# A kernel planner that may place GpSimd's sums and scalings on VectorE, and makes GpSimd wait for a VectorE operation that it held up

## The chip, the cores and the metric

The kernel runs on one core of a Trainium2 chip. The metric is the device time of one execution in microseconds, the median of several. The core's engines, by their names in the profile, are PE (TensorE, matrix products; PEld is its weight load), DVE (VectorE), ACT (ScalarE), POOL (GpSimd) and SP (SyncE, which issues the transfers). Each runs its own list of instructions in order, and they wait for each other by semaphores.

## What is computed

One layer of a bidirectional encoder over 2048 tokens of width 1024: windowed attention with 16 query heads and 4 key heads of width 64 (each query block of 128 tokens sees 384 keys), then a gated feed-forward part of width 2816. Around each part stand RMS norms and a shift, scale and gate from a conditioning vector. The reference, cut:

```python
mod = (silu(c) @ ada_w + ada_b);  sh1, sc1, g1, sh2, sc2, g2 = split(mod, 6)
h = rmsnorm(x, mix_norm_pre) * (1 + sc1) + sh1
q, k, v = split(h @ w_qkv)
logits = where(window, q @ k.T * dh**-0.5 + rel_bias, -1e30)
p = softmax(concat([logits, sink]))[..., :-1]
x = x + g1 * rmsnorm((p @ v) @ w_o, mix_norm_post)
h = rmsnorm(x, ffn_norm_pre) * (1 + sc2) + sh2
a, b = split(h @ ffn_w_in)
x = x + g2 * rmsnorm((silu(a) * b) @ ffn_w_out, ffn_norm_post)
```

All is float32. A product is made of three matmuls on rounded parts: each operand is split into `hi`, its rounded copy (made on ACT), and `lo`, the rest (a subtraction on DVE or POOL), and hi x hi, hi x lo and lo x hi are summed in a PSUM bank (`three`, line 782, and `split`, line 788).

## The kernel before

The kernel has two layers of code. `encoder_layer` (line 708) writes down the whole computation as a list of operations, each with a fixed engine. A recorder takes the list, a planner orders it, and the result is emitted; for this reason nearly every instruction carries the same line, 693, in the profile, and one goes by the names of the tiles.

*The work, in order of time.* (1) Norm, query, key and value products of the first chunk of 512 tokens, with the weights split as they come (`w_piece`, line 898, on POOL) and the modulation reduced on DVE (`ada`). (2) Attention in 64 units (`Unit`): four score products, a sum with the bias on DVE (`pr<-bank`), the exponential on ACT, a scaling of each of the four heads' rows by the reciprocal sum on POOL (`pr<-pr,rs`, line 1076), transposes on PE, ACT and DVE copies (`phi`, `plo`), the value product, and its reading from the bank (`low` on ACT, `of` on DVE). Between the units PE gets other work as filler: the remaining query, key and value products, then, from the middle on, the output projection (`ol`, `wo`) with its norms and residuals, whose sums (`y`, `yacc`, `xacc`, lines 1131 to 1146 and 1206) are POOL's. (3) The feed-forward's first product, in two halves of the tokens and 22 column tiles each. It is done with seven products instead of eight (a 2x2 block scheme): DVE makes sums and differences of weights (`s_i`, `wiri`), ACT and DVE split them (`ws_i`, `wa_i`), and DVE combines the seven results from the banks (`u_i`, `p_i`, `b_i`). POOL multiplies the two gates (`p_i<-p_i,u_i`, line 1443) and makes half of the differences for the next product (`differences`, line 1148). (4) The second product, in the same scheme and several parts (`ws_o`, `wa_o`, `z`); four of the final combinations of each block are POOL's (line 1572), the others DVE's. (5) Squares, norms, and the output (`zsq`, `nrz`, `zx`).

The PSUM banks are few: in attention two for the scores, three for the transposes, one for the value product and two for filler; in the feed-forward six.

*What sets the order.* `record` (line 176) gives each operation its costs (`cost`, line 233): the time for which it occupies its engine, its latency, and whether it uses the SBUF access that DVE and POOL share (`port`: every POOL operation except custom ones; on DVE, operations of over 128 columns with two SBUF inputs, and copies and scalings within SBUF). `forward` (line 330) plays the engines forward: each has a heap of operations that are ready (`now`) and of those that become ready (`soon`); the engine that can begin earliest takes its most urgent operation. An operation with `port` begins at the earliest 60 ns before the other engine's operation with `port` ends. `backward` (line 569) computes urgencies from the result, `replay` (line 509) plays an order again under random delays of the transfers, and `schedule` (line 632) repeats this 18 times and keeps the order with the shortest replay. `HOP` (line 75) is the planner's delay from one engine to another, 105 ns to POOL. `emit` (line 656) writes the instructions in that order, each on its engine; where the planner made one operation wait for another on purpose (`extra`), it adds a dependence.

So the planner knows that the two engines exclude each other, but in the program nothing says which goes first.

Of the kernel before, what the change touches and what calls it, by code (L numbers as in the profile page):

```python
# [76 lines left out]
class Op:  # L77
    __slots__ = ("i", "eng", "fn", "args", "kw", "reads", "writes", "occ", "lat", "port", "table", "tiles", "pred", "succ",
                 "start", "end", "put", "prio", "npred", "ready", "ins", "bytes",
                 "wire", "out", "wait", "extra")  # L80

# [52 lines left out]
class Recorder:  # L134
# [41 lines left out]
    def record(self, eng, fn, args, kw):  # L176
        op = Op()
# [14 lines left out]
        elif fn == "matmul":  # L192
            op.writes = [(op.writes[0][0], (3, (1 << P) - 1))]
        self.cost(op, [x for j, x in aps if j in out], [x for j, x in aps if j not in out])
        op.pred = {}
# [18 lines left out]
        self.ops.append(op)  # L214
        return op

    def gap(self, q, op):
# [112 lines left out]
    def forward(self, ahead, spare):  # L330
# [8 lines left out]
        for o in ops:  # L339
            o.npred, o.ready, o.put, o.wait, o.extra = len(o.pred), 0.0, 0, None, []  # L340
# [3 lines left out]
        port, moved = {"dve": 0.0, "pool": 0.0}, 0  # L344
        lanes, dma, table = [0.0] * 8, 0.0, None
# [20 lines left out]
        def offer(o):  # L366
            ready = o.ready
            for b in o.tiles:
# [8 lines left out]
        def drop(heap, o):  # L377
            if o in heap[0]:
                heapq.heappop(heap)
            else:  # L380
                heap.pop(next(k for k, x in enumerate(heap) if o in x))
                heapq.heapify(heap)

        def wake(t):
            for u in (t, *t.later):
                if u.parked:
                    again, u.parked = u.parked, []
                    for o in again:
                        offer(o)

        for o in ops:
            if not o.npred:
                offer(o)
        while n < len(ops):
            best = None
            for e in ENGINES:
                t, nw, sn = clock[e], now[e], soon[e]
                if e == "sp":
                    t = max(t, lanes[0])
                while sn and sn[0][0] <= t:  # L400
                    r, p, i, o = heapq.heappop(sn)
                    heapq.heappush(nw, (p, i, o, r))
                if nw:
                    item, begin, src = nw[0], t, nw
                elif sn:
                    item, begin, src = sn[0], sn[0][0], sn
                    item = (item[1], item[2], item[3], item[0])
                else:
                    continue
                o = item[2]  # L410
                ask = begin
                if o.port:
# [4 lines left out]
            if e == "dve" and o.port and src is now[e] and begin > clock[e] + 150:  # L417
                other = [x for x in now[e] if not x[2].port]
                if other:
                    item = min(other)  # L420
                    o, begin = item[2], clock[e]
                    ask = begin
            if ahead and e in ("act", "dve", "pool") and o.put < 4:
                wait, by = 0.0, None
                for g in (e, *({"dve": ("pool",), "pool": ("dve",)}.get(e, ()) if o.port else ())):
                    for r, p, i, y in soon[g]:
                        if g != e and not y.port:
                            continue
                        if r < begin + o.occ and max(begin - o.prio, begin + o.occ - p) > max(r - p, r + y.occ - o.prio) + 50:
                            w = r + (y.lat + HOP[e] if g != e else 1.0)  # L430
                            if w > wait:
                                wait, by = w, y if g != e else None
                if wait:
                    drop(src, o)
                    o.put += 1
                    if by is not None:
                        o.wait = by
                    heapq.heappush(soon[e], (wait, o.prio, o.i, o))
                    continue
            if e == "act" and o.table and o.table != table:  # L440
                stay = [x for x in now[e] if x[2].table in (None, table)]
                near = [x for x in soon[e] if x[3].table == table and x[0] < begin + 900]
                if stay and near:
                    item = min(stay)
                    o, src = item[2], now[e]
                elif near:
                    x = min(near)
                    item, src, o, begin = (x[1], x[2], x[3], x[0]), soon[e], x[3], max(begin, x[0])
            drop(src, o)
            again = False  # L450
# [10 lines left out]
            y = o.wait  # L461
            if y is not None and y.npred < 0 and max(clock[e], o.ready) <= y.start + 20:
                o.extra = [y]
                begin = max(begin, y.end + HOP[e])
            if e == "act" and o.table and o.table != table:
                table = o.table
                begin += 1283
# [10 lines left out]
            else:  # L478
                end = begin + o.lat
                if o.port:  # L480
                    port[e] = begin + o.occ
            o.npred = -1
            clock[e] = begin + o.occ + (late if e == "sp" else 0)
            o.start, o.end = begin, end
# [17 lines left out]
            for q in o.succ:  # L502
                q.npred -= 1
                q.ready = max(q.ready, begin if o.eng == q.eng == "pe" else end + (HOP[q.eng] if o.eng != q.eng else 30))
                if not q.npred:
                    offer(q)
# [125 lines left out]
    def schedule(self, rounds):  # L632
# [8 lines left out]
        for i in range(rounds):  # L641
# [4 lines left out]
            if best is None or real < best[1]:  # L646
                best = order, real, {b: b.slot for b in self.bufs.values()}, {o: o.extra for o in order if o.extra}
            if prio:
                for o in order:
                    o.prio = prio[o]  # L650
        self.slots, self.extra = best[2:]
        return best[0]
# [3 lines left out]
    def emit(self, nc, tc, order, outside):  # L656
# [1106 lines left out]
```

## Time and profile before

| | |
|---|---|
| median of 3 runs | 2058.2 us (2055.8 to 3376.76) |
| profiled execution, own time | 2063.44 us |
| its span, first to last instruction | 2061.7 us |
| granted TensorE clock, mean | 0.991 |
| instructions on DVE, ACT, POOL | 2933, 2122, 687 |
| DMA | 396.33 MB, mean 192 GB/s |

How to read it: the page gives busy times for the whole span; the windows view gives them by stretch, with the granted clock, and is what shows where PE is not busy; the view of waits and the timelines say what ended a gap. An arrow `<-` within brackets names what the engine waited for, with the time.

The chain of work that ended last goes through PE's matmuls for 54% of the span (936.73 us in one piece, from 870.39 us). POOL's instructions and their time by kind:

| POOL instruction | count | mean, ns |
|---|---|---|
| scaling `pr<-pr,rs`, 128x384 | 256 | 603 |
| small copy `pr<-nsink`, 128x4 | 64 | 237 |
| gate product `p_i<-p_i,u_i`, 128x512 | 44 | 1613 |
| gate product `u_i<-u_i,b_i`, 128x512 | 44 | 1483 |
| sums `z<-z,z`, 128x512 | 32 | 1586 |
| sums `yacc<-yacc,ysq`, 128x512 | 28 | 1420 |
| splits `w`, 128x896 and less | 16 | 2169 |
| splits `ol`, `ws`, `wo`, 128x1024 | 12, 12, 8 | 2438, 2408, 2404 |

### The profile page before, as it was taken

What the parts mean: (1) busy time and instruction counts of PE and PEld (TensorE: products, weight loads), DVE (VectorE), ACT (ScalarE), POOL (GpSimd) and SP (SyncE); (2) the same over time, 40 slices, a digit from 0 to 9 for tenths busy, and PEclk for the clock granted to TensorE, in tenths of its full rate; (3) what the DMA queues carried; (4) which work ended last, traced back from release to release, by engine and by line L of the source; (5) the groups of instructions that cost most, each with busy time, mean ns of one, the idle gap of its engine ahead of it and who ended that gap; (6) DMA issues with size and microseconds to landing.
All of it is one profiled execution on the core that took longest, in us unless ns stands there. A gap on an engine that the chain in (4) does not pass through costs nothing.

```text
span 2061.7 us, 28956 instructions
## 1 busy us (share of the span) xinstructions
PE 1998.0 (97%) x9366; PEld 1662.3 (81%) x9366; DVE 1659.1 (80%) x2933; ACT 1081.5 (52%) x2122; POOL 735.5 (36%) x687
## 2 busy tenths in 40 slices
PE   6999999999998999999999999999999999979997
PEld 4888888888787778888888888888888888858886
DVE  7867877765568889887878999776666799989998
ACT  5557766777687864344333633333333744455432
POOL 3413544466978624433435322222221000220030
PEclk9999999999999999999999999999999999999999
DMA  8895765486786695444446843432333554346543
GB/s 296 300 336 198 250 206 197 169 299 214 239 279 215 227 351 170 169 156 171 155 159 228 291 147 136 140 124 91 118 112 112 165 169 164 129 131 242 174 152 108
DMA packets 201667, 396.33 MB, mean 192 GB/s; under 512 B 19195, under 2 KB 61228, under 8 KB 198444
## 3 DMA queue, kind: packets, MB, share of 16 engines
q1 hardware_dynamic: 200940, 393.97, 55.7%
q8 instruction: 74, 1.21, 0.2%
q14 instruction: 77, 0.63, 0.1%
q10 hardware_dynamic: 576, 0.52, 0.1%
HBM read 270.65 MB, written 123.76 MB: 191 GB/s over the span
## 4 chain that ended last, share of the span: by engine, by line
PE 54%; DVE 2%; issue 1%; ACT 1%; POOL 0%; DMA 0%; DVEq 0%; ACTq 0%; POOLq 0%
PE bank L693 54%; DVE z L693 1%; DVE zx L693 1%; ACT nrz L693 0%; POOL z L693 0%; DVE ntz L693 0%; DMA hb22o<-g_d_b 0%; DVE ws_o L693 0%; DVE s_o L693 0%; DVE nrz L693 0%; ACT ws_o L693 0%; ACT zsq L693 0%; POOL p_i L693 0%; DVE zacc L693 0%; ACT L687 0%
## 5 line engine op out<-in xcount | busy, mean ns | idle before, releaser
L693 PE MATMUL bank<-ht,ws_i 128*128 128x512 f32 x1584 | 373.6, 389 | 0.0
L693 PEld LDWEIGHTS bank<-ht,ws_i 128*128 128x128 f32 x1584 | 297.4, 188 | 61.7
L693 PE MATMUL bank<-hb,wa_i 128*128 128x512 f32 x1056 | 254.7, 389 | 0.0
L693 PEld LDWEIGHTS bank<-hb,wa_i 128*128 128x128 f32 x1056 | 198.3, 188 | 41.1
L693 PE MATMUL bank<-ol,wo 128*128 128x512 f32 x768 | 204.0, 397 | 2.2 <-DVE ol L693 1.1
L693 DVE CUSTOM_DVE_ANT_0 pr<-bank,bias,nsink 128x384 f32<-128x384 f32 (+1 forms) x256 | 149.3, 596 | 56.8 <-PE bank L693 55.0
L693 POOL TENSOR_SCALAR pr<-pr,rs 128x384 f32<-128x384 f32 (+1 forms) x256 | 149.7, 603 | 121.6 <-DVE rs L693 115.5
L693 ACT ACTIVATE pr<-pr,nm 128x385 f32<-128x385 f32 (+1 forms) x256 | 154.9, 606 | 71.4 <-DVE nm L693 68.4
L693 POOL TENSOR_TENSOR p_i<-p_i,u_i 128x512 f32<-128x512 f32 x44 | 70.9, 1613 | 311.0 <-ACT wa_i L693 125.9
L693 ACT CAST ws_i<-s_i 128x512 fp32r<-128x512 f32 x132 | 81.9, 620 | 183.1 <-DVE s_i L693 92.9
L693 POOL TENSOR_TENSOR z<-z,z 128x512 f32<-128x512 f32 x32 | 50.2, 1586 | 357.4 <-issue 151.7
L693 DVE TENSOR_TENSOR u_i<-bank,u_i 128x512 f32<-128x512 f32 x176 | 120.7, 688 | 62.5 <-PE bank L693 61.9
L693 PEld LDWEIGHTS bank<-ol,wo 128*128 128x128 f32 x768 | 142.8, 189 | 29.4 <-DVE ol L693 1.5
L693 DVE TENSOR_TENSOR plo<-bank,phi 128x512 fp32r<-128x512 f32 x184 | 120.9, 686 | 30.9 <-ACT phi L693 28.6
L693 PE MATMUL bank<-k,q 128*128 128x384 f32 (+1 forms) x512 | 135.5, 346 | 3.7 <-DVE nm L693 3.7
L693 PE MATMUL bank<-hi,ws 128*128 128x512 f32 x384 | 134.5, 399 | 0.0
L693 DVE TENSOR_TENSOR wa_i<-wiri,wa_i 128x512 fp32r<-128x512 f32 x132 | 114.6, 868 | 21.1 <-ACT wa_i L693 18.4
L693 PE MATMUL bank<-hb,ws_i 128*128 128x512 f32 x528 | 127.0, 389 | 0.6 <-ACT p_i L693 0.6
L693 PE MATMUL bank<-ht,wa_i 128*128 128x512 f32 x528 | 127.0, 389 | 0.0
L693 ACT CAST wa_i<-wiri 128x512 fp32r<-128x512 f32 x132 | 81.1, 620 | 74.3 <-PE bank L693 70.4
L693 DVE TENSOR_TENSOR z<-bank,z 128x512 f32<-128x512 f32 (+1 forms) x164 | 107.6, 661 | 13.3 <-PE bank L693 12.7
L693 PEld LDWEIGHTS bank<-hb,ws_i 128*128 128x128 f32 x528 | 99.1, 188 | 21.5 <-ACT p_i L693 1.0
(245 smaller groups left out, 4526.7 us busy)
## 6 DMA issues: line engine op xcount, KB each, us to landing
wiri<-w_in SPq DMA_DIRECT2D x88, 512.0 KB, 4.7
ada<-ada_w SPq DMA_DIRECT2D x40, 512.0 KB, 5.0
wiro<-w_out SPq DMA_DIRECT2D x48, 384.0 KB, 3.9
q_d<-e SPq DMA_DIRECT2D x32, 512.0 KB, 4.0
q<-q_d SPq DMA_DIRECT2D x16, 1024.0 KB, 6.5
wo<-wo_d SPq DMA_DIRECT2D x16, 1024.0 KB, 5.5
g_d_b<-p_i SPq DMA_DIRECT2D x44, 256.0 KB, 3.4
g_d_t<-p_i SPq DMA_DIRECT2D x40, 256.0 KB, 2.0
```

Source lines behind the costliest of these rows:

```text
L693: o.ins = getattr(engs[o.eng], o.fn)(*args, **kw)
```

## The change

Three things change, all in the planner; `encoder_layer` stays as it is, so the operations and their results are the same.

1. Each `tensor_tensor` and `tensor_scalar` that is written for POOL gets a second form on DVE, with DVE's cost (`others`, and `forms` in `record`). A ready operation stands in both engines' heaps. When DVE is about to take one, `sooner` looks whether POOL, after the more urgent work in its heap, would end it earlier; if so, DVE leaves it for later. When POOL is about to take one, nothing is compared. At equal times DVE is asked before POOL. Nothing moves from DVE to POOL, and transfers, ACT and PE keep their operations.
2. `turn`: where an operation with `port` on DVE was held up by more than 100 ns in the plan, the next operation with `port` on POOL gets a dependence on it, if POOL came free no more than 100 ns after that operation began and would itself begin after it.
3. The chosen engine of each operation is kept with the best order (`self.at`) and used in `emit`. A stamp on heap entries voids the copies of an operation that was offered again.

```diff
+        op.forms, op.calls, op.stamp = {}, {}, 0
+        for op.eng, op.fn, op.args, op.kw in (*self.others(eng, fn, args, kw, ins), (eng, fn, args, kw)):
+            self.cost(op, outs, ins)
+            op.forms[op.eng] = op.occ, op.lat, op.port, op.table
+            op.calls[op.eng] = op.fn, op.args, op.kw
+        op.eng_first = eng
...
+    def others(self, eng, fn, args, kw, ins):
+        if eng == "pool" and fn in ("tensor_tensor", "tensor_scalar"):
+            yield "dve", fn, args, kw
...
-            heapq.heappush(soon[o.eng], (ready, o.prio, o.i, o))
+            for e in o.forms:
+                heapq.heappush(soon[e], (ready, o.prio, o.i, o, o.stamp))
...
+        def sooner(o, e, begin):
+            end = begin + o.forms[e][1]
+            for f, (occ, lat, _, _) in o.forms.items():
+                if f != e:
+                    t = max(clock[f], o.ready)
+                    for p, i, y, r, k in now[f]:
+                        if p < o.prio and y.npred >= 0 and k == y.stamp:
+                            t += y.forms[f][0]
+                            if t + lat >= end:
+                                break
+                    if t + lat < end:
+                        return t
+            return None
...
+            if len(o.forms) > 1 and e != o.eng_first:
+                t = sooner(o, e, begin)
+                if t is not None:
+                    later(max(begin, t) + 100)
+                    continue
...
+            if e == "pool" and uses and not o.extra and turn is not None and clock[e] - 100 < turn.start < begin:
+                o.extra = [turn]
+                begin = max(begin, turn.end + HOP[e])
+            if e == "dve" and uses:
+                turn = o if begin > ask + 100 else None
...
+                o.eng = self.at[o]
+                o.table = o.forms[o.eng][3]
+                o.fn, o.args, o.kw = o.calls[o.eng]
```

More of the change, by code (lines that the diff above doesn't have):

```diff
@@ L79 @@
                  "start", "end", "put", "prio", "npred", "ready", "ins", "bytes",
-                 "wire", "out", "wait", "extra")
+                 "wire", "out", "wait", "extra",
+                 "forms", "calls", "stamp", "eng_first")
 class Buf:
@@ L339, in forward @@
         for o in ops:
-            o.npred, o.ready, o.put, o.wait, o.extra = len(o.pred), 0.0, 0, None, []
+            o.npred, o.ready, o.put, o.wait, o.extra, o.stamp = len(o.pred), 0.0, 0, None, [], 0
         clock = dict.fromkeys(ENGINES, 700.0)
@@ L416, in forward @@
             begin, ask, e, o, src, item = best
-            if e == "dve" and o.port and src is now[e] and begin > clock[e] + 150:
-                other = [x for x in now[e] if not x[2].port]
+            if e == "dve" and o.forms[e][2] and src is now[e] and begin > clock[e] + 150:
+                other = [x for x in now[e] if not x[2].forms[e][2] and x[4] == x[2].stamp and x[2].npred >= 0]
                 if other:
@@ L478, in forward @@
             else:
-                end = begin + o.lat
-                if o.port:
-                    port[e] = begin + o.occ
+                end = begin + lat
+                if uses:
+                    port[e] = begin + occ
             o.npred = -1
-            clock[e] = begin + o.occ + (late if e == "sp" else 0)
+            o.eng, o.occ, o.lat, o.port, o.table = e, occ, lat, uses, tab
+            clock[e] = begin + occ + (late if e == "sp" else 0)
             o.start, o.end = begin, end
@@ L503, in forward @@
                 q.npred -= 1
-                q.ready = max(q.ready, begin if o.eng == q.eng == "pe" else end + (HOP[q.eng] if o.eng != q.eng else 30))
+                q.ready = max(q.ready, begin if e == q.eng == "pe" else
+                              end + (HOP[q.eng] if len(q.forms) > 1 or e != q.eng else 30))
                 if not q.npred:
@@ L646, in schedule @@
             if best is None or real < best[1]:
[L647 removed]
+                best = (order, real, {b: b.slot for b in self.bufs.values()}, {o: o.extra for o in order if o.extra},
+                        {o: o.eng for o in order})
             if prio:
```

73 lines of the change are left out of this document (41 added, 32 removed).

## The prediction

> **What bounds the kernel now.** I read the page first, then the windows view by stage, then TensorE's waits, then the timelines around its longest gaps.
>
> ```profile
> span 2061.7 us, 28956 instructions
> PE 1998.0 (97%) x9366; PEld 1662.3 (81%) x9366; DVE 1659.1 (80%) x2933; ACT 1081.5 (52%) x2122; POOL 735.5 (36%) x687
> ...
> 0.00:160.00 160.00, 137.83 (x649) 111.32 (x650) 115.38 (x176) 86.96 (x143) 50.04 (x34) 0.99 0.87 306
> 160.00:560.00 400.00, 396.09 (x2100) 339.25 (x2098) 284.75 (x730) 294.24 (x670) 227.60 (x289) 1.00 0.66 224
> 560.00:730.00 170.00, 157.95 (x801) 130.40 (x801) 133.35 (x286) 131.94 (x292) 120.25 (x144) 0.97 0.70 241
> 870.00:1800.00 930.00, 929.61 (x4101) 769.85 (x4102) 763.62 (x1160) 384.70 (x681) 244.46 (x162) 1.00 0.45 154
> 1800.00:1860.00 60.00, 47.60 (x184) 36.22 (x183) 53.75 (x92) 33.75 (x64) 12.67 (x7) 0.89 0.43 134
> 1860.00:2062.00 202.00, 189.08 (x920) 159.79 (x919) 184.01 (x334) 82.73 (x164) 23.56 (x16) 0.97 0.50 170
> ```
>
> In a windows row stand the length, then the busy time of PE, PEld, DVE, ACT and POOL, the granted clock, the DMA share and GB/s. TensorE is the bound: 1998.0 of 2061.7 us, idle only 63.7. From 870 to 1800 us it is busy 929.61 of 930 at clock 1.00: nothing that POOL or DVE does there can shorten it. What can move are the holes: 160 - 137.83 = 22.2 us at the head, 12.0 us in late attention (560 to 730), 12.4 us at 1800 to 1860 and 12.9 us in the last stretch. POOL counts only where its work, or the SBUF access it shares with DVE, opens a hole.
>
> **The change, part by part.** The planner may put each of the 687 POOL instructions that is a two-input sum, difference or product, or a scaling, on DVE. Prices:
>
> ```profile
> L693 POOL TENSOR_TENSOR p_i<-p_i,u_i 128x512 f32<-128x512 f32 x44 | 70.9, 1613 | 311.0 <-ACT wa_i L693 125.9 <-DVE u_i L693 87.8 <-ACT u_i L693 17.0
> L693 POOL TENSOR_TENSOR ws<-wsr,ws 128x1024 fp32r<-128x1024 f32 x12 | 28.9, 2408 | 20.9 <-ACT ws L693 20.9
> L693 POOL TENSOR_SCALAR pr<-pr,rs 128x384 f32<-128x384 f32 (+1 forms) x256 | 149.7, 603 | 121.6 <-DVE rs L693 115.5 <-DMA wor<-w_o 2.8 <-DVE nloo L693 1.7
> ...
> L693 DVE TENSOR_TENSOR ws_i<-s_i,ws_i x132: 675/686/1782, 724.1 to 1561.0; 128x512 fp32r<-128x512 f32 x132
> L693 DVE TENSOR_TENSOR wo<-wor,wo 128x1024 fp32r<-128x1024 f32 x8 | 10.9, 1359 | 3.1 <-ACT wo L693 3.1
> L693 DVE TENSOR_SCALAR nta<-nta x4: 419/428/429, 19.6 to 176.4; 128x512 f32<-128x512 f32 x4
> ```
>
> The tile rows give minimum/median/maximum in ns. A 512-column sum falls from 1613 to 686 ns (ratio 0.43), a 1024-column split from 2408 to 1359 (0.56), a scaling from 603 to at most 428 (0.71; DVE's scaling by a column is not shown, so it lies between that row and POOL's 603; I take 428, the same operation). Also, a sum on POOL that touches a DVE operation with two SBUF inputs holds it: ws_i's median is 686 and its maximum 1782, one hold of 1.1 us.
>
> How much moves follows from the planner's rule: on a tie DVE is asked first, and refuses only where POOL would end sooner; with DVE busy and POOL free, POOL takes it. DVE is idle 115 of 400 us at 160 to 560, so I expect about a third to move, most where POOL is backed up.
>
> *Long middle, 870 to 1800.* Cost zero; the cover is TensorE's 929.61. Were all 162 POOL instructions moved at 0.686, DVE would have 763.62 + 111 = 875 of 930 us, still under it, before the holds that vanish. With that cover gone it would cost the excess, which is none.
>
> *The wait.* POOL now waits for a two-input DVE operation that it has held up in the plan. One place in the trace is this:
>
> ```profile
> 623.62 7.85 DVE L693 TENSOR_TENSOR s_i<-wiri,s_i 128x512 f32<-128x512 f32 x1
> ...
> 623.52 1.27 POOL L693 TENSOR_TENSOR y<-y,xr 128x512 f32<-128x512 f32 x1
> 624.77 2.50 POOL L693 TENSOR_TENSOR y<-y,no 128x512 f32<-128x512 f32 x2
> 627.23 1.25 POOL L693 TENSOR_TENSOR xacc<-xacc,xsq 128x512 f32<-128x512 f32 x1
> 628.45 2.47 POOL L693 TENSOR_TENSOR y<-y,xr 128x512 f32<-128x512 f32 x2
> ...
> 632.38 0.77 PE L693 MATMUL bank<-phi,v 128*128 128x512 f32 x1 [6.43 <-DVE of L693]
> 632.94 0.63 PE L693 MATMUL bank<-plo,v 128*128 128x512 f32 x1
> ...
> 624.00:640.00 16.00, 9.57 (x44) 7.71 (x44) 14.31 (x19) 7.34 (x16) 7.36 (x7) 0.79 0.43 134
> ```
>
> s_i, due after one POOL instruction, ends at 631.47, 0.55 us after POOL's sixth in a row ends at 630.92. Behind it on DVE stands the reading of the attention bank, and TensorE loses 6.43 us; then it runs at a mean clock of 0.79, worth 9.57 x 0.21 = 2.0 us. With the hold cut to one POOL instruction, s_i takes 1.78, so 7.85 - 1.78 = 6.07 of the 6.43 goes, and the clock with it: **-8.0** (bounds 0 and -8.4).
> The Trainium skill, page "SBUF — State Buffer", section "Who interferes with whom", says that whichever of the two issues first has the shared ports for its whole instruction and the other blocks until that one has finished. By that, s_i would have gone in after the first sum, the wait would buy nothing, and the sum below would be -4 instead of -12; this row, six instructions long, disagrees.
>
> *Other holes with POOL in the chain.*
>
> ```profile
> 550.00:566.00 16.00, 11.45 (x46) 7.97 (x45) 8.41 (x18) 9.71 (x20) 15.05 (x15) 0.89 0.65 213
> 664.00:682.00 18.00, 15.47 (x80) 11.58 (x80) 15.42 (x37) 14.05 (x36) 12.93 (x19) 1.00 0.38 126
> 720.00:732.00 12.00, 9.81 (x42) 7.48 (x41) 9.71 (x10) 5.08 (x8) 5.67 (x4) 1.00 1.04 384
> ...
> 556.70 0.63 ACT L693 ACTIVATE xsq<-y 128x512 f32<-128x512 f32 x1 [1.38 <-POOL y L693]
> ...
> 1813.17 4.96 POOL L693 TENSOR_TENSOR z<-z,z 128x512 f32<-128x512 f32 x2 [4.37 <-DVE z L693]
> 1816.93 1.15 ACT L693 ACTIVATE zsq<-z 128x512 f32<-128x512 f32 x2 [1.93 <-POOL z L693]
> 1818.53 0.74 PE L693 MATMUL bank<-ht3o,ws_o 128*128 128x512 f32 x2 [2.49 <-ACT ws_o L693]
> 1851.56 0.69 ACT L693 ACTIVATE nrz<-bank,epsc 128x512 f32<-128x512 f32 x1 [2.35 <-DVE z L693]
> 1855.68 1.22 PE L693 MATMUL bank<-hb11o,wa_o 128*128 128x512 f32 x2 [7.09 <-ACT wa_o L693]
> ```
>
> At 550 to 566 POOL is full (15.05 of 16) and DVE half idle; ScalarE sat 1.38 us behind POOL's y with the attention copies queued after it, and TensorE lost 4.55 us plus 11.45 x 0.11 = 1.3 of clock. I take **-2** (0 to -5.8). At 664 to 682 and 720 to 732 TensorE lost 2.5 and 2.2 us; DVE is the fuller engine, so **-1** (0 to -4.7). At 1813 two z sums take 4.96 us on POOL where DVE needs twice 0.69; ScalarE's square, and the weight cast behind it, wait 1.93, and TensorE 2.49. I take **-3**, that hole and half a us of slow clock (0 to -5.3: all of the stretch's 12.4 but the 7.09 of the last row). That larger hole, at 1855.68, waits for ScalarE behind DVE's finishing work; no POOL instruction is in it: 0.
>
> ```profile
> 30.68 2.62 POOL L693 TENSOR_TENSOR w<-wqkv,w 128x896 fp32r<-128x896 f32 x1 [3.28 <-DVE mod L693]
> ...
> 31.25 3.12 DVE L693 CUSTOM_DVE_ANT_0 ada<-ada,cb,adab 128x1024 f32<-128x1024 f32 x1
> ...
> 35.05 0.79 PE L693 MATMUL bank<-lo,w 128*128 128x512 f32 x1 [2.38 <-DVE lo L693]
> ```
>
> At the head a weight split holds DVE's ada, and TensorE waits 2.38 for the DVE operation after it. The transfers (share 0.87) limit the head too: **-1** (0 to -2.4).
>
> *What it adds.* POOL's wait costs nothing where POOL is idle (64% of the span). What is queued behind it are the pr scalings, which TensorE's transposes await. Only around 550 to 566 is there no slack: each of 15 instructions could wait once for a 0.686 operation plus the planner's 0.105 hop, 12 us; a quarter is **+3** (0 to +12). No transfer changes its queue: SP keeps issuing them, in a newly planned order, and POOL's queue holds none. DVE's queue gets longer by what moves; its price is rival 3.
>
> Sum: -8 - 2 - 1 - 3 - 1 + 3 = **-12**, on the profiled execution's own 2063.4 us (span 2061.7 and 1.7 around it): 2051.4. The median of the runs, 2058.2, lies 5.2 below that execution: I predict **2046 us**.
>
> **The rivals.**
> 1. *The hold was not POOL's alone, or another takes its place.* Were the access handed over after each POOL instruction, s_i's 7.85 would have another cause and term one would be nil: -4, 2054 us. For it: ws_i's 132 instructions never wait for more than one. Against: s_i ends with POOL's run. That the planner moves too little to matter gives the same.
> 2. *All holes with POOL in the chain close:* -8.4 - 5.8 - 4.7 - 5.3 - 2.4 = -26.6, 2032 us; a new order that also closes the 7.09 hole gives 2024. DVE's 53.75 of 60 us there speaks against it.
> 3. *Slower: DVE's queue is blocked by what was moved.* DVE runs in order, and attention has few banks. POOL's own waits, harmless now:
>
> ```profile
> POOL ws L693 <- ACT ws L693: 20.9, 7, 6.5
> POOL ol L693 <- ACT ol L693: 8.2, 3, 4.5
> POOL wo L693 <- ACT wo L693: 5.2, 3, 2.6
> ```
>
> These 34.3 us (total, times, longest), taken to DVE ahead of bank reads, would stop TensorE. Moving all of POOL's 120.25 us at 560 to 730 would, at 0.43 to 0.71, put 52 to 85 us on DVE's 133.35 of 170, past the stretch by 15 to 48. If half of the waits land: +17, 2075; all, with the extra 15: +49, 2107. It outweighs the gains once more than a third of the waits (12 us) lands. Against it: the planner gives DVE only what it can begin when free.
>
> **How the numbers follow.** Forecast 0.52, rival 1 0.18, rival 2 0.10, rival 3 0.20. The likeliest gives 2046, its own range 2032 (rival 2's sum) to 2054. The range 2022 to 2070 reaches below to rival 2 with the 7.09 hole and 2 us of clock behind it, above to no gain plus the +12; outside are about 0.05 below and 0.14 above. Two per cent, about what a measurement of this kernel can tell from no change, is 41 us. Faster needs nearly every hole closed: 0.04, from rival 2. Slower needs rival 3 beyond its whole 34.3 us of waits: 0.06. The rest, 0.90, is within.
>
> **What would show it.** Right: no DVE row beyond about 2 us between 160 and 730 us apart from 1024-column ones; POOL's count clearly under 687 and DVE's above 2933; TensorE in the late attention at least 10 us less idle or slowed; z at 1813 on DVE; the middle still full. Wrong: a hold of several us again, a TensorE gap released by DVE where a moved sum stands in front, or any hole in the middle stretch.

## The result, and the profile after

| | before | after |
|---|---|---|
| median of 11 runs, us | 2062.92 (2055.19 to 3376.76) | 2051.82 (2050.53 to 2055.14) |
| profiled execution, own time, us | 2063.44 | 2052.78 |

The ratio is 0.9959, with a 95% interval of 0.9943 to 0.9975, which is of the means and makes 8.5 us; it lies within the two per cent. The single run of 3376.76 us is in no ratio; the median of the other ten is 2060.56. The kernel before was timed again beside the changed one, and its median is now 2062.92, not 2058.2. That difference matters below: its times lie in two groups. In the longest row of them on one chip, 9 of 32 lie between 2054.72 and 2057.19 and 23 between 2061.56 and 2067.62, with nothing between (on two other chips single times do lie between, as 2059.27, 2060.56 and 2060.85). The changed kernel's times have one group.

The page of the changed kernel, then its windows view over the stretches that the prediction showed up to 1860 us and the one left out there, 730 to 870:

```profile
span 2051.0 us, 28847 instructions
PE 1996.0 (97%) x9366; PEld 1661.0 (81%) x9366; DVE 1716.2 (84%) x3114; ACT 1081.7 (53%) x2122; POOL 561.0 (27%) x506
...
0.00:160.00 160.00, 138.40 (x664) 112.99 (x665) 118.30 (x191) 88.28 (x144) 25.42 (x20) 1.00 0.89 312
160.00:560.00 400.00, 395.97 (x2095) 338.68 (x2094) 336.04 (x825) 296.71 (x679) 170.74 (x206) 0.99 0.66 223
560.00:730.00 170.00, 165.18 (x843) 137.30 (x843) 147.98 (x330) 135.29 (x291) 92.18 (x104) 0.99 0.77 265
730.00:870.00 140.00, 138.15 (x602) 113.57 (x601) 123.14 (x164) 63.41 (x107) 45.50 (x31) 0.99 0.54 192
870.00:1800.00 930.00, 929.42 (x4101) 769.52 (x4100) 762.46 (x1194) 386.11 (x683) 193.97 (x128) 1.00 0.45 155
1800.00:1860.00 60.00, 50.48 (x196) 37.86 (x195) 51.84 (x94) 35.42 (x68) 10.45 (x4) 0.91 0.45 144
```

181 instructions went from POOL (687 to 506) to DVE (2933 to 3114), about a quarter. The span is 10.7 us shorter (2061.7 to 2051.0): TensorE's idle time falls by 8.7 us (63.7 to 55.0) and its busy time by 2.0 (1998.0 to 1996.0).

In late attention the idle time falls from 12.05 to 170 - 165.18 = 4.82 us. The clock there rises from 0.97 to 0.99, which would be 157.95 x 0.03 - 165.18 x 0.01 = 3.1 us; a second profile of the changed kernel has 0.98 and 165.30 us, which makes 1.4. The clock's part is known no better than that. From 1800 to 1860 the idle time falls from 12.40 to 9.52, at the head from 22.17 to 21.60. The middle is as full as it was, and after 1860 the idle time is 12.6 us in both.

Most of the gain in late attention is the hold of `s_i`: with one wait alone, below, the same stretch gains 5.6 us of idle time. At the other places there that the prediction priced, TensorE still waits. Two windows and two rows of the changed kernel, then a row of the kernel before:

```profile
550.00:566.00 16.00, 13.11 (x52) 9.73 (x52) 13.74 (x35) 10.93 (x25) 11.67 (x12) 0.79 0.86 291
700.00:720.00 20.00, 17.45 (x74) 13.16 (x73) 17.61 (x21) 13.01 (x21) 6.46 (x4) 1.00 1.04 401
```

```profile
554.57 0.55 PE L747 MATMUL bank<-ident,pr 128*128 128x128 f32 x3 [1.21 <-DVE pr L747]
...
714.76 1.43 PE L747 MATMUL bank<-ol,wo 128*128 128x512 f32 x5 [1.07 <-ACT yacc L747]
```

```profile
726.29 6.87 PE L693 MATMUL bank<-ol,wo 128*128 128x512 f32 x29 [1.07 <-ACT yacc L693]
```

From 550 to 566 TensorE loses 2.89 us in place of 4.55, but at a clock of 0.79 in place of 0.89, so 13.11 x 0.21 = 2.8 us in place of 1.3: 5.6 us together against 5.8. One of its gaps there, 1.21 us, now ends with a scaling on DVE. The hole at 720 to 732 has only come earlier: the same products of `ol` and `wo` wait for the same `yacc`, and 2.55 us are lost from 700 to 720 where 2.2 were lost before. From 664 to 682 nothing is lost any more, but 1.92 us are from 640 to 660, where the kernel before lost nothing.

From 730 to 870 the change loses: before, TensorE was busy 139.84 of these 140 us, now 138.15. The window before; TensorE's own row in the changed kernel stands last, and above it the rows of the chain of waits that lead to it:

```profile
730.00:870.00 140.00, 139.84 (x617) 115.48 (x616) 124.25 (x158) 67.19 (x113) 56.96 (x38) 1.00 0.64 222
```

```profile
834.26 3.90 DMA ly<-y_d
838.23 1.30 POOL ly L747
839.55 0.70 DVE ly L747
840.28 0.63 ACT xsq L747
840.91 0.48 ACT p_i L747
```

```profile
841.43 4.57 PE L747 MATMUL bank<-hb,ws_i 128*128 128x512 f32 x12 [1.84 <-ACT p_i L747]
```

A load that lands at 838.16 is followed by a sum on POOL, one on DVE, a square on ACT, and behind that square in ACT's queue stands the copy that empties a bank: 1.84 us that the kernel before did not lose. The four stand so in the newly planned order; at this place the kernel before had no gap.

The moved scalings, by tile, then the `z` sums in the groups of POOL, then two rows of DVE's timeline in attention:

```profile
L747 POOL TENSOR_SCALAR pr<-pr,rs x177: 472/593/1742, 168.9 to 686.8; 128x384 f32<-128x384 f32 x153, 128x256 f32<-128x256 f32 x24
L747 DVE TENSOR_SCALAR pr<-pr,rs x79: 338/423/2374, 168.8 to 681.3; 128x384 f32<-128x384 f32 x71, 128x256 f32<-128x256 f32 x8
```

```profile
L747 POOL TENSOR_TENSOR z<-z,z 128x512 f32<-128x512 f32 x32 | 50.6, 1588 | 354.4 <-issue 151.2 <-ACT ws_o L747 117.7 <-DVE z L747 76.8
```

```profile
381.31 2.37 DVE L747 TENSOR_SCALAR pr<-pr,rs 128x384 f32<-128x384 f32 x1
...
702.09 1.78 DVE L747 TENSOR_TENSOR hf<-y,hf 128x512 f32<-128x512 f32 x1
```

The hold of 7.85 us is gone: in attention, from 160 to 730 us, DVE's longest instruction of up to 512 columns is the first of these rows, a scaling of 2.37 us in place of 0.42. All 32 `z` sums are still POOL's. Around 1803 us:

```profile
1803.33 6.55 POOL L747 TENSOR_TENSOR z<-z,z 128x512 f32<-128x512 f32 x2 [3.90 <-DVE z L747]
...
1808.65 1.16 ACT L747 ACTIVATE zsq<-z 128x512 f32<-128x512 f32 x2 [2.18 <-POOL z L747]
...
1811.05 1.20 PE L747 MATMUL bank<-ht1o,ws_o 128*128 128x512 f32 x4 [0.94 <-DVE ws_o L747]
...
1845.77 1.22 PE L747 MATMUL bank<-hb11o,wa_o 128*128 128x512 f32 x2 [6.10 <-ACT wa_o L747]
```

ACT's square waits for POOL's `z` as before (2.18 us; it was 1.93). TensorE's gaps in this stretch without the large one come to 12.40 - 7.09 = 5.31 us before and to 9.52 - 6.10 = 3.42 now. The large one, in which no POOL instruction stands, takes 6.10 us in place of 7.09 here, but 7.06 in a second profile of the changed kernel, so that this part may be chance.

### The profile page after: what moved, and what is told of

It reads as the page before. It is cut to its first block, busy times and chain, and to the rows that moved or that the text cites. A ratio compares the mean times of both kernels' runs of the same rounds, so it can differ in the third digit from the quotient of the medians.

```text
span 2051.0 us, 28847 instructions
## 1 busy us (share of the span) xinstructions
PE 1996.0 (97%) x9366; PEld 1661.0 (81%) x9366; DVE 1716.2 (84%) x3114; ACT 1081.7 (53%) x2122; POOL 561.0 (27%) x506
## 3 DMA queue, kind: packets, MB, share of 16 engines
q8 instruction: 74, 1.21, 0.2%
## 4 chain that ended last, share of the span: by engine, by line
PE 59%; DVE 6%; DMA 1%; issue 1%; ACT 1%; POOL 1%; SPq 0%; DVEq 0%; ACTq 0%; POOLq 0%
PE bank L747 59%; DVE z L747 1%; DVE zx L747 1%; POOL z L747 0%; DMA hb<-h_d 0%; DVE pr L747 0%; DVE plo L747 0%; DMA wor<-w_o 0%; DVE s_o L747 0%; DVE zacc L747 0%; DVE u_i L747 0%; DMA ht2o<-g_d_t 0%; DVE ws_o L747 0%; ACT nrz L747 0%; DMA ly<-y_d 0%
## 5 line engine op out<-in xcount | busy, mean ns | idle before, releaser
L747 POOL TENSOR_SCALAR pr<-pr,rs 128x384 f32<-128x384 f32 (+1 forms) x177 | 115.5, 665 | 179.8 <-DVE rs L747 168.1
L747 DVE TENSOR_TENSOR plo<-bank,phi 128x512 fp32r<-128x512 f32 x184 | 120.8, 684 | 10.2 <-ACT phi L747 9.0
L747 DVE TENSOR_TENSOR wa_i<-wiri,wa_i 128x512 fp32r<-128x512 f32 x132 | 107.0, 812 | 19.0 <-ACT wa_i L747 18.9
```

Of the source, the lines that this page charges most:

```text
L747: o.ins = getattr(engs[o.eng], o.fn)(*args, **kw)
```

## The experiments

The theories. **A:** the hold of `s_i` is worth most of the gain, and the new waits remove it (the prediction's). **B:** it is the placement on DVE that is worth the gain, with or without waits. **C:** neither; every planning yields another order, orders differ by as much as the gain, and the new one is merely a better one. Ratios are to the kernel before, timed on the same chip; below 1 is faster.

**One wait alone.** The kernel before, in its own order, with one dependence more: POOL's second `y` sum waits for `s_i`.

```diff
+        held = next(o for o in best[0] if o.eng == "dve" and any(x.name == "s4_i0_0" for x, _ in o.writes))
+        after = next(o for o in best[0] if o.eng == "pool" and [x.name for x, _ in o.reads[:2]] == ["y1_2", "no1"])
+        self.extra[after] = [*self.extra.get(after, ()), held]
```

> The kernel before, same order and same engines, with one dependence added: POOL's second residual product of the run at 624 us (y<-y,no) waits for the one DVE operation s_i that was held for 7.85 us. Theory A (the gain of the change is this hold, taken away by its waits): s_i takes under 2.5 us, TensorE's 6.43 us gap behind it goes with the slow clock after it, and the time falls by 6 to 9 us, ratio about 0.996 to 0.997 against before. Theory B (the gain is the placement on DVE) and theory C (it is only that a new order fell out better): the ratio is 1.000 within 0.001, since nothing is placed or ordered anew.

Measured: 2056.37 us (2053.95 to 2059.16, 12 runs), against 2062.24; ratio 0.998 [0.9968, 0.9992]. DVE's row of `s_i`, POOL's rows around it, and the window of late attention:

```profile
623.88 1.55 DVE L696 TENSOR_TENSOR s_i<-wiri,s_i 128x512 f32<-128x512 f32 x1
```

```profile
623.60 1.28 POOL L696 TENSOR_TENSOR y<-y,xr 128x512 f32<-128x512 f32 x1
625.51 2.53 POOL L696 TENSOR_TENSOR y<-y,no 128x512 f32<-128x512 f32 x2 [0.63 <-DVE s_i L696]
```

```profile
560.00:730.00 170.00, 163.53 (x830) 134.64 (x829) 129.07 (x291) 134.65 (x297) 122.73 (x146) 0.99 0.74 255
```

`s_i` takes 1.55 us in place of 7.85, POOL gives up 0.63 us, TensorE's idle time in this stretch goes from 12.05 to 6.47, and all twelve times lie near the lower group of the kernel before. So the hold goes with the upper group; no execution of the unchanged kernel in the lower group was profiled. Its price is 2063.44 - 2056.77 = 6.7 us between the two profiled executions, 5.9 between the medians. Of the 6.7, 5.1 is TensorE's idle time (63.7 to 58.6) and 1.6 its busy time (1998.0 to 1996.4).

**The waits alone.** The kernel before, in its own order and on its own engines, with the dependences that the change's rule finds when applied to it (79 of them).

```diff
+            o.turn = None
+            if e == "pool" and o.port and not o.extra and turn is not None and clock[e] - 100 < turn.start < begin:
+                o.turn = turn
+            if e == "dve" and o.port:
+                turn = o if begin > ask + 100 else None
...
+        for o, q in turns.items():
+            self.extra[o] = [*self.extra.get(o, ()), q]
```

> The kernel before, same order and engines, with all the waits that the change's rule would give on that order (79 more dependences of POOL on a held DVE operation). Theory A: as with the one wait, 0.996 to 0.997, and the other 78 add or take less than 2 us. Theory B and C: 1.000. If the waits cost POOL something in the late attention, the time is 3 to 10 us above the kernel with one wait.

Measured: 2063.4 us (2056.95 to 2066.33, 12), ratio 1.0009 [0.9994, 1.0024]: nothing. The times are in two groups again, 4 by 2057 and 8 from 2062.53 up. DVE's row and POOL's, in its profile:

```profile
625.15 7.83 DVE L701 TENSOR_TENSOR s_i<-wiri,s_i 128x512 f32<-128x512 f32 x1
```

```profile
624.99 1.32 POOL L701 TENSOR_TENSOR y<-y,xr 128x512 f32<-128x512 f32 x1
626.23 2.55 POOL L701 TENSOR_TENSOR y<-y,no 128x512 f32<-128x512 f32 x2
```

The hold is there, and POOL's `y<-y,no` waits for nothing. The rule acts on a DVE operation that was held up in the plan. In the plan of the kernel before, `s_i` went first and was not held up by more than the rule's 100 ns; on the chip POOL went first. So the rule adds 79 waits and misses the one place that had a price.

**The changed kernel without its waits.** Same order, same engines; the 96 dependences of the new rule are left out of the program.

```diff
+                o.tied = True
...
-        self.slots, self.extra, self.at = best[2:]
+        self.slots, self.extra, self.at, tied = best[2:]
+        self.extra = {o: q for o, q in self.extra.items() if o not in tied}
```

> The changed kernel, with its own order and engines, but without its 96 new dependences of POOL on DVE. Theory A: somewhere in attention a DVE operation is held over several POOL instructions again (a row above 3 us) and 3 to 8 us of the gain are lost, ratio 0.998 to 1.000 against before. Theory B and C: the order and the engines carry the gain, ratio 0.996 as the changed kernel, no difference without the waits.

Measured: 2053.09 us (2050.9 to 2055.71, 9), ratio 0.9961 [0.9946, 0.9975], as good as the changed kernel's 0.9959, and no long hold came back. The waits buy nothing that can be measured here, and cost nothing.

**Planned without the rule.** The planner chooses engines as in the change, but never adds the new dependence, so it also finds another order.

```diff
-                turn = o if begin > ask + 100 else None
+                turn = None
```

> The planner with both forms but without the rule of the wait, so planned anew. Theory A: near the kernel before, 0.998 to 1.001, with at least one long hold on DVE. Theory B: 0.996 or less. Theory C: anything between 0.993 and 1.003, with the holes of TensorE at other places than in both kernels.

Measured: 2055.65 us (2053.91 to 2058.55, 12), ratio 0.9974 [0.9961, 0.9987]; the longest DVE instruction of up to 512 columns in attention takes 2.48 us. Theory A falls in its second half: the hold costs 6.7 us of the 10.7 by profile, but it is not the waits that remove it. The new orders do: in none of their profiles is an `s_i` held by a run of POOL sums.

**Other orders of both planners.** Each planner keeps the best of 18 orders by its replay. These four kernels take the second or the third best, and change nothing else.

```diff
-            if best is None or real < best[1]:
-                best = order, real, {b: b.slot for b in self.bufs.values()}, {o: o.extra for o in order if o.extra}
+            found.append((order, real, {b: b.slot for b in self.bufs.values()}, {o: o.extra for o in order if o.extra}))
...
+        best = sorted(found, key=lambda x: x[1])[1]
```

(with `[2]` for the third; in the changed planner the same, with the engines kept beside each order)

> The planner of before, unchanged, but of its 18 orders the second best instead of the best. Theory C (orders of one planner differ on the chip by as much as the change moved the time): the ratio against before lies anywhere within 0.994 and 1.004, with TensorE's holes at other places. Theory B (placement on DVE is worth about 4 us beyond the hold): it is not under 0.998, and a kernel that has no hold of several us lies within 0.1% of the one with one wait added (2056 us).

> The planner of the change, but of its 18 orders the second best. Theory B: within 2 us of the changed kernel, ratio 0.995 to 0.997. Theory C: it may as well be at 0.998 to 1.002, on the orders of before.

> The planner of before, third best of its 18 orders. As for the second: theory B no lower than 0.998; theory C anything from 0.994 to 1.004.

> The planner of the change, third best of its 18 orders. Theory B: 0.995 to 0.997. Theory C: up to 1.002, and the three orders of each planner overlap.

Measured, all four on one chip, where the kernel before had 2064.38 (19 runs):

| order | old planner | new planner |
|---|---|---|
| best | 1 (by definition) | 0.9959 [0.9943, 0.9975] |
| second | 2066.76 us, 1.0004 [0.999, 1.0018] | 2057.24 us, 0.9966 [0.9954, 0.9978] |
| third | 2055.32 us, 0.9958 [0.9946, 0.997] | 2058.5 us, 0.9974 [0.9963, 0.9984] |

The old planner's third order, with all 687 instructions still on POOL, is as fast as the change. The longest `s_i` in DVE's timeline of the second one, then of the third, and the third's window of late attention:

```profile
622.32 4.00 DVE L693 TENSOR_TENSOR s_i<-s_i,wiri 128x512 f32<-128x512 f32 x1
```

```profile
639.12 2.66 DVE L693 TENSOR_TENSOR s_i<-wiri,s_i 128x512 f32<-128x512 f32 x1
```

```profile
560.00:730.00 170.00, 165.02 (x834) 136.73 (x835) 133.66 (x295) 133.94 (x295) 121.60 (x144) 0.98 0.74 257
```

The second order of the old planner again holds an `s_i`, for 4.00 us, and its times spread from 2057.44 to 2071.28. In the third the longest takes 2.66; its late attention is as full (165.02) as that of the changed kernel (165.18), with POOL busy 121.60 us there instead of 92.18. So what the changed kernel shows in late attention can be had without moving anything. This is theory C, as far as it goes: the three orders of each planner overlap, and three are too few to say whether the new planner's are better on the average. What all profiles of plans with a choice of engines have in common is that no `s_i` takes over 2 us (the longest 1.80); two of the old planner's three orders hold one for 4 us or more.

**The placement alone, both ways.** In the order of the kernel before, the same 181 instructions are put on DVE; and in the order of the changed kernel, its 181 are put back on POOL. Nothing is planned anew.

```diff
+        for o in best[0]:
+            if o.i in MOVED:
+                o.eng = "dve"
+        self.extra = {o: [q for q in qs if q.eng != o.eng] for o, qs in self.extra.items()}
```

```diff
+        self.at = {o: o.eng_first for o in best[0]}
+        self.extra = {o: [q for q in qs if self.at[q] != self.at[o]] for o, qs in self.extra.items()}
```

> The order of the kernel before, with the same 181 instructions put on DVE that the change put there, and no new waits. Theory B (the placement has a worth of its own, about 4 us): 0.996 or less, also because a shorter run of POOL instructions cannot hold DVE for 7.85 us. Theory C (orders differ, the placement itself is worth nothing): 0.998 to 1.000 where the hold goes, as with the one wait. If instructions that now stand in DVE's queue where they were not planned block it, it is slower than before, above 1.002.

> The order of the changed kernel, with its 181 instructions put back on POOL. Theory B: the gain goes, 0.999 to 1.004, and TensorE waits for POOL's scalings in attention. Theory C: the order carries it, 0.996 to 0.997.

Measured: 2069.36 us (2066.03 to 2070.52, 10), ratio 1.0041 [1.0026, 1.0057], for the first; 2067.93 us (2066.69 to 2069.39, 12), ratio 1.0041 [1.0027, 1.0055], for the second. TensorE's waits (total, times, longest, in us) and the window of late attention, of the first kernel and then of the second, and after them the like waits in the order of before with one wait:

```profile
PE bank L710 <- DVE nm L710: 5.0, 6, 3.2
PE bank L710 <- DVE plo L710: 4.0, 9, 0.9
PE bank L710 <- DVE of L710: 3.6, 4, 1.7
```

```profile
560.00:730.00 170.00, 159.68 (x790) 128.68 (x790) 147.54 (x336) 133.09 (x294) 89.42 (x100) 0.96 0.67 233
```

```profile
PE bank L749 <- POOL pr L749: 10.2, 12, 2.5
```

```profile
560.00:730.00 170.00, 159.16 (x799) 128.78 (x799) 119.59 (x283) 133.79 (x294) 124.73 (x150) 0.98 0.73 250
```

```profile
PE bank L696 <- DVE nm L696: 3.7, 3, 2.7
PE bank L696 <- DVE of L696: 1.2, 1, 1.2
```

Both lose in attention, and the releaser says why. With the instructions moved and the order kept, the hold is gone (that `s_i` takes 1.78 us), but TensorE waits for DVE's reading of its banks (`nm`, `plo`, `of`), behind which the moved work now stands in front: 12.6 us, against 5.3 in the same order with the one wait, which has no hold either and 0.4 for `plo`. That is the prediction's third rival. With the order kept and the instructions put back, it waits 10.2 us for POOL's scalings, against 1.2 in the changed kernel. These waits are not the whole loss: TensorE's busy time grows as well, from 1996.4 to 2003.0 and from 1996.0 to 2000.8 us. Theory B falls: the placement has no worth that can be added to another order. Order and engines fit each other; separated, they cost 0.4% against the kernel before, and more against the same orders whole (0.998 with one wait, 0.9959 the changed kernel).

**`z` on DVE.** The prediction expected the two `z` sums at 1813 us to go to DVE and to bring 3 us. They stayed, so here all 32 are written for DVE, and the changed planner plans the rest.

```diff
-                (pool if (i, x) in ((2, 2), (4, 4), (5, 5), (6, 6)) else dve).tensor_tensor(sums[hf, n2, x], sums[hf, n2, x], sums[hf, n2, y], ALU.add)
+                dve.tensor_tensor(sums[hf, n2, x], sums[hf, n2, x], sums[hf, n2, y], ALU.add)
```

> The changed kernel, planned anew with the 32 z sums written for DVE, so that none stays on POOL. By the prediction's step on the z sums: no POOL instruction at 1800 to 1830, ScalarE's square no longer waits for POOL there, TensorE's holes at the sums go (0.9 and 1.8 us in the changed kernel) with the slow clock after them, 3 us in all, ratio 0.993 to 0.995 against before. If those holes have other causes (DVE is full there), the stretch keeps its 10 us of lost time and the ratio is 0.995 to 0.998, within the spread of orders.

Measured: 2050.97 us (2048.93 to 2055.53, 7), ratio 0.9952 [0.9932, 0.9971]. The changed kernel was not on that chip, so both ran again, side by side (the changed kernel without any edit):

> The changed kernel beside the others on this chip: 2051 to 2054 us, in one group, no row of DVE above 3 us in attention.

> The changed kernel with the z sums written for DVE, on the same chip as the changed kernel. If the sums on POOL cost what the prediction took, it is 2 to 4 us under the changed kernel; if the difference seen so far is the chip, less than 1 us.

Measured: 2053.62 us (2050.76 to 2054.18, 10), ratio 0.9967 [0.9954, 0.998], for the changed kernel, and 2050.96 us (2049.08 to 2052.58, 7), ratio 0.9954 [0.9938, 0.9969], with `z` on DVE. The means are 2.5 us apart, about 1.2 either way. The stretch from 1800 to 1860, of the changed kernel's second profile and of the other:

```profile
1800.00:1860.00 60.00, 49.30 (x192) 36.70 (x191) 52.22 (x95) 34.91 (x67) 10.45 (x4) 0.91 0.44 140
```

```profile
1800.00:1860.00 60.00, 51.48 (x209) 40.61 (x210) 53.78 (x98) 37.90 (x73) 0.00 (x0) 0.94 0.49 163
```

TensorE's idle time goes from 10.70 to 8.52 us, and its slowness by the clock from 49.30 x 0.09 = 4.4 to 51.48 x 0.06 = 3.1 (in the first profile with `z` on DVE it is 51.25 x 0.09 = 4.6, so the clock's part is not sure). DVE has 53.78 us of work in 60 and still has room for the sums. This kernel has the lowest median of the study.

Not all of the 2.5 us is the sums', since the plan is a new one. ACT's copies of the second product's results (minimum, median and maximum in ns, then the first and last start in us), of the changed kernel's second profile and of the other:

```profile
L747 ACT COPY z<-bank x56: 566/587/605, 1591.8 to 1877.6; 128x512 f32<-128x512 f32 x56
```

```profile
L747 ACT COPY z<-bank x56: 565/589/605, 1588.6 to 1873.2; 128x512 f32<-128x512 f32 x56
```

The first POOL sum of `z` starts at 1751.0 us. At 1590 the kernel with `z` on DVE is already 3.2 us ahead, of the 5.1 by which the two spans differ in the end (2052.4 and 2047.3); between the first profiles of the two kernels it is 1.7 (1591.4 and 1589.7) of 3.2. So 1.5 to 1.9 us of these profiles come where the sums are; the rest is another order, or chance.

**Who goes first.** If the hold comes from POOL having begun before `s_i`, then making `s_i` wait for POOL's first sum should bring it into every execution. The order is that of the kernel before.

```diff
+        first = next(o for o in order if o.eng == "pool" and [x.name for x, _ in o.reads[:2]] == ["y1_1", "xr1_1"])
+        order.remove(first)
+        order.insert(order.index(held), first)
+        self.extra[held] = [*self.extra.get(held, ()), first]
```

> The kernel before, with the DVE operation s_i at 624 us made to wait for the POOL sum beside which it stands, so that it always comes to the shared access while POOL has its next instructions in hand. If the hold makes the two groups of times in which the kernel before runs (2055 to 2057 and 2061 to 2067 us), then all of this kernel's runs lie in the upper group, as those with the one wait all lay in the lower one (2054 to 2059): ratio 1.001 to 1.002, and a row of 5 to 8 us for s_i. If the groups have another cause, they show here too.

Measured: 2063.8 us (2056.55 to 2067.25, 12: 3 up to 2058.46, 9 from 2063.28 up), ratio 1.0008 [0.9993, 1.0022]. The two groups are still there, so the expectation was missed. Its profiled execution took 2056.91, one of the lower group; DVE's row and POOL's:

```profile
626.31 1.77 DVE L699 TENSOR_TENSOR s_i<-wiri,s_i 128x512 f32<-128x512 f32 x1 [1.10 <-POOL y L699]
```

```profile
625.00 1.27 POOL L699 TENSOR_TENSOR y<-y,xr 128x512 f32<-128x512 f32 x1
626.24 2.96 POOL L699 TENSOR_TENSOR y<-y,no 128x512 f32<-128x512 f32 x2
```

Here POOL had gone first and had another sum waiting, and `s_i` still went in after one instruction: it ended at 628.08, and POOL's pair took 2.96 us where 2.50 is usual. The upper nine times are those that the hold gives, though none of these executions was profiled. The profiles of this order agree: 2063.44 and 2064.27 us with the hold (7.85 and 7.83), 2056.91 without. So one program, with the same two queues, most likely has executions with the hold and without it. What decides between them stays open.

## Why the prediction was right and where it failed

Two steps failed, one in the mechanism and one in the number.

**The mechanism: "With the hold cut to one POOL instruction, s_i takes 1.78, so 7.85 - 1.78 = 6.07 of the 6.43 goes, and the clock with it: -8.0".** The prediction let the change's wait do the cutting. It does not: the same rule on the old order leaves the hold at 7.83 us, and the changed kernel without its waits does not have it either (0.9961 and 0.9959). The prediction took the order on the chip (POOL first) for the order in the plan, and the rule sees only the plan. What removed the hold is a newly planned order, which the prediction did not count as a cause of this.

**The number: "The median of the runs, 2058.2, lies 5.2 below that execution: I predict 2046 us."** The sum stood on the profiled execution, which had the hold. The median and the lowest of the runs, 2058.2 and 2055.8, lie in or beside the lower group, where there is no hold to remove. Taking 8 us for the hold off a time that does not contain it made the forecast 5.2 us too low.

On the profiled execution itself the sum gave 2051.4; measured are 2052.78 in the profile and 2051.82 in the median. That it comes so near is luck: the sum has 1.3 us too much for the hold, 3 us for places that lost as much after the change as before, and 3 us for an event that did not happen, and against them +3 for a wait that cost nothing, and nothing for what the new order brought.

Step by step:

- *The hold, -8.* The place and the cause (POOL's run of sums beside `s_i`) were right, shown by one dependence that removes it. The size is 6.7 us by profile, 5.9 by median. That the change's wait would cut it was wrong.
- *550 to 566, -2.* The place lost 5.8 us with its slow clock and loses 5.6 now.
- *The two holes at 664 and 720, -1.* They lost 2.5 and 2.2 us. Now 1.92 are lost from 640 to 660 and 2.55 from 700 to 720. So of the 7.2 us of idle time that late attention gained, hardly any is from this term and the one above.
- *`z`, -3.* The event did not come: the planner left all 32 on POOL. The prediction itself says that with DVE busy and POOL free POOL takes the work, and it quotes DVE's 53.75 of 60 us there under the second rival; it did not apply this to the step. Where the sums were put on DVE by hand, 2.5 us came (give or take 1.2), of which the profiles put 1.5 to 1.9 where the sums are. What the stretch gained in the changed kernel instead, 2.9 us of idle time, came with the new order, and 1.2 us of it is not there in a second profile.
- *The wait, +3.* It costs nothing measurable: 0.9961 without it, 0.9959 with it. The loss came elsewhere, at 841 us (1.84 us), in a stretch that was full before and that the prediction did not look at.
- *Head, -1, and middle, 0.* The head gained 0.6 us; the middle is at 929.42 of 930.
- *What moves.* About a third was expected, 181 of 687 moved. The prices on DVE were those taken only where nothing holds the instruction: a scaling has a median of 423 ns against the 428 taken, but its mean is no better than POOL's 603 before:

```profile
L747 DVE TENSOR_SCALAR pr<-pr,rs 128x384 f32<-128x384 f32 x71 | 42.7, 614 | 1.3
```

Of the signs that it named for being right, POOL's count and the full middle came. The longest DVE row is 2.37 us instead of about 2; late attention gained 7.2 us of idle time and 1.4 to 3.1 by the clock where at least 10 was asked; `z` at 1813 did not come. Of the signs for being wrong, one came in a small way: the gap of 1.21 us at 554 us that a moved scaling on DVE ends.

The rivals: the first (the access handed over after each instruction) fits some executions and not others, as far as the last experiment shows, on the old order with one dependence more. The third (DVE's queue blocked) is what the same move does without a new plan, +0.4%; the planner avoids most of it. The second did not come: 6.10 us of the large hole (7.06 in a second profile) and most of the small ones are left.

Not settled: how much of the changed kernel's gain beyond the hold belongs to the choice of engines, and how much to a lucky order. Three orders of each planner, from 0.9958 to 1.0004 and from 0.9959 to 0.9974, overlap. By profile the changed kernel is 4.0 us shorter than the old order with one wait (spans 2051.0 and 2055.0). By stretch, TensorE's idle time is 0.3 us less at the head, 1.5 less from 160 to 730 and 3.6 less from 1800 to 1860, and 1.9 more from 730 to 1800.

## What to carry to other kernels

Before a gain is taken off a median, ask whether the median's runs contain the event that the profile shows: here a profiled stall of 6 to 7 us was, by the two groups of times, in only some of the executions. When a planner's rule is changed, compare a few orders of the old planner first, since another order alone moved this kernel by 0.4%. A rule that acts on what happens in the plan cannot mend what happens only on the chip: 79 waits from the plan did nothing, and one that was read from the trace took the stall away.

## What the runs showed of the hardware

The Trainium skill, page "SBUF — State Buffer", section "Who interferes with whom", has the shared access held, for its whole instruction, by whichever of the two engines issues first. Most rows agree: held sums on DVE mostly stop near 1.78 us, the 686 ns alone and 1.1 us of one POOL sum, and the scaling of 2.37 us above ends 0.2 us after one POOL split of 1024 columns. Four rows do not: 7.85 and 7.83 us for `s_i` beside a run of six POOL sums, and 4.00 and 2.66 in two other orders. It also goes the other way round. In the changed kernel the chain has one POOL sum of 512 columns, otherwise 1.6 us long with its waiting, at

```profile
1803.33 5.30 POOL z L747
```

and DVE's timeline has no gap in that time, down to

```profile
1806.79 0.68 DVE L747 TENSOR_TENSOR ht4o<-ht4o 128x512 fp32r<-128x512 f32 x1
```

which ends at 1807.47, 1.16 us before POOL's sum does at 1808.63, about one such sum alone (1.27). A second profile of the changed kernel has such a sum of 5.30 us too. So an engine with a full queue can keep the other out for several of its instructions, on either side. On DVE's side it does not come in every execution, if the two groups of times are read rightly, and there it is worth some 6 us of 2060.

Does moved work also save DVE some of its waiting? In the order of the changed kernel with all 181 instructions back on POOL, the page's line of busy times reads

```profile
PE 2000.8 (97%) x9366; PEld 1661.4 (80%) x9366; DVE 1626.1 (79%) x2933; ACT 1081.6 (52%) x2122; POOL 727.0 (35%) x687
```

At the medians, the 79 scalings (423 ns), 18 small copies (172 ns) and 84 others (686 ns or more) are at least 94 us of work by estimate. In the new order the move adds 90.1 us to DVE's busy time (1626.1 to 1716.2), so it saved DVE little. In the old order it adds 69.2 (1659.1 to 1728.3), so 25 us or more were saved, some 6 of them the hold's. The new order alone, with nothing moved, saves 33 (1659.1 to 1626.1). TensorE, the bound, did not gain by either alone: both of these kernels are 0.4% slower than the one before.
